# Tile-by-tile pool handover, one pass over K, and Q and K written two chunks at a time in a hybrid decoder step

## The chip, the cores and the metric

The kernel runs as one program on one core of one Trainium2 chip. The metric is the device time of one execution, in microseconds (us). Times of the kernel before and of the changed one are medians of several executions; the profile shows one more execution, recorded by the hardware profiler.

## The reference, cut to what matters

The program is one inference step of a small decoder with two layers, in float32, for a prompt of 1024 tokens and, at the same time, 8 sequences that each decode one token against 256 cached positions (two cached pages of 128 per sequence). All 1032 tokens go through the same weights.

```python
for l in range(DEPTH):                      # two layers
    if l < N_A_LAYERS:                      # layer 0: short gated convolution
        y, st = short_conv_mixer(x, conv_state[l], w_in[l], conv_w[l], w_mix_out[l])
    else:                                   # layer 1: differential attention
        kv = x @ w_kv
        k_new = partial_rope(kv[..., :QK_DIM].reshape(N, T, N_HEADS, 2, HEAD_DIM), pos)
        v_new = kv[..., QK_DIM:].reshape(N, T, N_HEADS, V_DIM)
        q = partial_rope((x @ w_q[i]).reshape(N, T, N_HEADS, 2, HEAD_DIM), pos)
        ...                                 # prompt: causal blocks; decode: past pages + new key
        a = p[:, :, 0] - lam * p[:, :, 1]   # two softmax maps per head
        o = rms_norm(a @ v, subln_g[i]) * (1.0 - lam_init)
        y = o.reshape(N, T, VO_DIM) @ w_o[i]
    x = layer_norm(DEEPNORM_ALPHA * x + y, ln1_g[l], ln1_b[l])
    x = layer_norm(DEEPNORM_ALPHA * x + swiglu(x, w_gate[l], w_up[l], w_down[l]), ln2_g[l], ln2_b[l])
```

The outputs are the new x of all tokens, k_new and v_new of all tokens, and the convolution states.

## The kernel before

**Layout.** The residual stream is held transposed: features on the 128 partitions (8 groups), tokens along the row, in four chunks of 258 tokens (CH). Chunk 3 ends with the 8 decode tokens. A float32 product is made of three products of split numbers: each operand is a high part (hi, rounded) and a low part (lo, the rest), and high x high, high x low and low x high are summed in PSUM (exact, lines 331 to 337). So one block, one chunk times one weight column group (dense, line 342), is 24 TensorE instructions of 258 columns. ScalarE makes hi by a cast (L166 for weights, L353 or L729 for data) and GpSimd (weights, L167) or VectorE (data, L354 or L730) makes lo by a subtraction.

**Weights.** A Stream (line 101) loads each half of a weight by a DMA on SP's queue into one of a few raw buffers and prepares hi and lo ahead of use into a ring. The main stream has a ring of 4; the stream of the stage that makes q, k and v has a ring of 8 and 3 raw buffers (line 1274). Resident (line 181) keeps a few weights for several uses.

**Stages.** The convolution mixer, FFN 0, then q (16 blocks for chunks 0 and 1, 16 for chunks 2 and 3), then k, then v for two of four pairs of heads, then attention by head (with the rest of v filled in), the output projection, FFN 1. K has two passes over its eight weights: chunk 3 alone, then chunks 0, 1 and 2 (line 1228). Every stage opens its own tile pools (open_pools, line 1200) in an ExitStack and closes them at its end, so that the next stage's pools lie over the same addresses. A pool opened in the default way has its tiles wait until all tiles of the earlier pools under it are released.

**q and k.** qk_op (line 743) runs one block and finishes it. Rows t = 0 and t = 1 hold the rotary halves: t = 0 is only copied (x1), t = 1 computes both rotated halves with six VectorE operations (L753 to L759). put (line 724) splits a chunk into hi and lo, in single-chunk buffers (3 of each), and writes both to DRAM on SP's queue, for k also the unsplit k (k_out). Attention later reads qh, ql, kh and kl per head.

**Decode** runs as a generator (line 826) beside the blocks of k and v: after each block side.step lets it go on until its next `yield "op"`, or for four bare yields. It gathers 16 cached K pages by indirect DMAs on GpSimd's queue (L862) into rf, which held the residual stream until that was written away to stash; multiplies each by the query (L884) and reduces it (L886); waits until the new key is complete (k_done); does a softmax; then multiplies 16 gathered V pages by their weights (L943), adds them in pairs (L947), and lets TensorE sum each pair over positions (od, L938). A gather waits until VectorE has finished with the page whose buffer it overwrites. decode_out (line 962) adds the new value, and needs all four pairs of v for the decode tokens (v_done).

**Order.** The program is written in this order, but a planner (the tile framework's scheduler, with its own costs) lays out each engine's queue from it, so an instruction can be hoisted over earlier ones of the same engine. On the chip each queue then runs strictly in the laid-out order.

Of the kernel before, what the change touches and what calls it, by code (L numbers as in the profile page):

```python
# [9 lines left out]
F32 = mybir.dt.float32  # L10
F32R = mybir.dt.float32r
# [6 lines left out]
P = 128  # L18
# [6 lines left out]
NCH = 4  # L25
HALF = ((0, 1), (2, 3))
CH = NTOK // NCH
# [209 lines left out]
def _chunk(c):  # L237
    return slice(c * CH, (c + 1) * CH)
# [3 lines left out]
def kernel(ctx: ExitStack, tc: tile.TileContext, xT, wts, prm, st, cst, dcst, rope, maskw, cache_k, cache_v,  # L242
                          page_table, y_out, k_out, v_out, conv_out):
    nc = tc.nc
    V, A, G, T, S = nc.vector, nc.scalar, nc.gpsimd, nc.tensor, nc.sync
# [34 lines left out]
    def block(items, f):  # L280
        prog.append((items, f))

    def half(*keys):
        return [("half", k) for k in keys]

    kept = {}

    def pair(key=None):

        for res in kept.values():  # L290
            if key in res.keys:
                return res.get(key)
        return [ws.take(), ws.take()]
# [4 lines left out]
    pools = {}  # L298
# [6 lines left out]
    def mm(n=CH):  # L305

        if "S" in pools:
            if not wide:
                for _ in range(2):
                    t = pools["S"].tile([P, 2, 512], F32, tag="S", name="mm2")  # L310
                    wide.extend((t[:, 0], t[:, 1]))
                wide.extend((None, None))
            t = wide.pop(0)
            if t is not None:
                return t[:, 0:n]
        t = pools["mm"].tile([P, 512], F32, tag="mm", name="mm")
        return t[:, 0:n]
# [7 lines left out]
    def tmp2():  # L325
        return pools["t2"].tile([P, CH], F32, tag="t2", name="t2")
# [15 lines left out]
    def dense(ps, w, c):  # L342

        exact(ps, [(cut(w[k // KP], k % KP), (xh[c][:, k], xl[c][:, k])) for k in range(KT)])
        return ps

    def need(c):
        g = lnq.pop(c, None)
        if g is not None:
            side.drain(g)  # L350

    def split_into(hi, lo, src):
        A.copy(out=hi, in_=src)  # L353
        V.tensor_tensor(out=lo, in0=src, in1=hi.bitcast(F32), op=ALU.subtract)  # L354

    order = {}
    tpool = None
# [139 lines left out]
    def ffn(l):  # L497
# [84 lines left out]
        final = [(n, l, f) for f in (NF - 2, NF - 1) for n in ("gate", "up")] + [("down", l, NG - 1, 0)]  # L582

        def keep_final():
            tpool.close()
            kept["ffn"] = Resident(nc, wts, tpool.enter_context(tc.tile_pool(name="kept", bufs=1)), final)

        def needs(*keys):
            return half(*[k for k in keys if k not in final])
# [128 lines left out]
    dec = {}  # L718

    def rows(t, n):  # L720

        return scr[n].rearrange("(m t i) n -> t m i n", t=8, i=8)[t]

    def put(c, t, src, which):

        hi = pools["qk"].tile([P, CH], F32R, tag="hi", name="hi")
        lo = pools["qk"].tile([P, CH], F32R, tag="lo", name="lo")
        if which == "q":
            A.activation(out=hi, in_=src, func=AF.Copy, scale=-0.125)  # L729
            V.scalar_tensor_tensor(out=lo, in0=src, scalar=-0.125, in1=hi.bitcast(F32),  # L730
                                   op0=ALU.mult, op1=ALU.subtract)
        else:
            split_into(hi, lo, src)
        S.dma_start(out=rows(t, which + "h")[:, :, _chunk(c)], in_=hi.bitcast(F32))
        S.dma_start(out=rows(t, which + "l")[:, :, _chunk(c)], in_=lo.bitcast(F32))
        if c == NCH - 1:
            V.tensor_copy(out=dec[which][:, t], in_=src[:, CH - DEC:])
            if t == 7:
                dec[which + "_done"] = True
        if which == "k":  # L740
            S.dma_start(out=k_out.rearrange("(m t i) n -> t m i n", t=8, i=8)[t][:, :, _chunk(c)], in_=src)

    def qk_op(which, t, c, w):
        need(c)
        ps = dense(mm(), w, c)
        if t == 0:
            dec["x1", c] = pools["t2"].tile([P, CH], F32, tag="x1", name="x1", bufs=2)
            A.copy(out=dec["x1", c], in_=ps)
        elif t == 1:
            x1 = dec["x1", c]  # L750
            cos, sin = dec["rope"][:, 0, _chunk(c)], dec["rope"][:, 1, _chunk(c)]
            o1, o2, t1, t2 = tmp2(), tmp2(), tmp2(), tmp2()
            V.tensor_tensor(out=t1, in0=ps, in1=sin, op=ALU.mult)  # L753
            V.tensor_tensor(out=t2, in0=ps, in1=cos, op=ALU.mult)
            V.tensor_tensor(out=o1, in0=x1, in1=cos, op=ALU.mult)
            V.tensor_tensor(out=o1, in0=o1, in1=t1, op=ALU.subtract)
            put(c, 0, o1, which)
            V.tensor_tensor(out=o2, in0=x1, in1=sin, op=ALU.mult)
            V.tensor_tensor(out=o2, in0=o2, in1=t2, op=ALU.add)  # L759
            put(c, 1, o2, which)  # L760
        elif which == "k":
            kf = tmp2()
            A.copy(out=kf, in_=ps)
            put(c, t, kf, which)
        else:
            put(c, t, ps, which)
        side.step(RATE)

    def produce(which, passes):
        def f(t, chunks):  # L770
            w = pair()
            for c in chunks:
                qk_op(which, t, c, w)
        for chunks in passes:
            for t in range(8):
                block(half((which, t)), lambda t=t, chunks=chunks: f(t, chunks))
# [49 lines left out]
    def decode():  # L826
# [23 lines left out]
        for half in range(2):  # L850
            tp = pools["st"].tile([P, 512], F32, tag="st", name="rt")
            for j in range(4):
                T.transpose(tp[0:DEC, j * P:(j + 1) * P], dec["q"][:, half * 4 + j], ident)
            A.copy(out=row.rearrange("b (m t i) -> b t m i", t=8, i=8)[:, half * 4:half * 4 + 4],
                   in_=tp[0:DEC].rearrange("b (t m i) -> b t m i", t=4, i=8))
# [18 lines left out]
        def query(b):  # L874
            A.dma_start(out=qbs[b % 2], in_=qrow_d[b].partition_broadcast(P))

        query(0)
        for j, (b, pg) in enumerate(pairs):
            if j + ahead < 16:
                gather(kv[(j + ahead) % 6], cache_k, *pairs[j + ahead])  # L880
            if pg == 0 and b + 1 < DEC:
                query(b + 1)
            t, qb = kv[j % 6], qbs[b % 2]
            V.tensor_tensor(out=t, in0=t, in1=qb, op=ALU.mult)  # L884
            yield "op" if pg else None
            V.tensor_reduce(out=sc[:, pg, 16 * b:16 * b + 16], in_=t.rearrange("p (m d) -> p m d", d=HD), axis=AX.X,  # L886
                            op=ALU.add)
        vv = kv + qbs
# [37 lines left out]
        for pg in range(2):  # L926
# [3 lines left out]
                        in_=tp[:, 0:PAST].rearrange("p (g c) -> p g c", c=2), axis=AX.X, op=ALU.add)  # L930
# [10 lines left out]
        for j, (b, pg) in enumerate(pairs):  # L941
            t = vv[j % 8].rearrange("p (h e) -> p h e", e=VD)
# [256 lines left out]

    def open_pools(stack, *specs):  # L1200
        for name, bufs, kw in specs:
            pools[name] = stack.enter_context(tc.tile_pool(name=name, bufs=bufs, **kw))

    def ffn_space(stack):

# [12 lines left out]
    def items(*parts):  # L1218
        return [i for q in parts for b in q for i in b[0]]
# [5 lines left out]
    produce("q", HALF)  # L1225
    part_q = part()
    early_q, part_q = part_q[:2], part_q[2:]
    produce("k", ((3,), (0, 1, 2)))
    fours = [half(("v", two, 0), ("v", two, 1)) for two in range(4)]
    n_k = len(prog)  # L1230
    for two in range(EARLY):
# [4 lines left out]
    part_k = part()  # L1236
# [6 lines left out]

    with ExitStack() as outer:
        open_pools(outer, ("r", 1, {}), ("s", 1, {}), ("t", 3, {}), ("mm", 6, PS), ("st", 2, PS))
        rf = pools["r"].tile([P, NCH, KT, CH], F32, name="rf")
        V.memset(eps_t, EPS)
        V.memset(mhalf, -0.5)
        A.activation(out=nlam, in_=eps_t, func=AF.Silu)
        ws = main  # L1250
        ws.start(2)
        for c in range(NCH):
            r[c] = rf[:, c]
            for k in range(0, KT, 2):
                S.dma_start(out=r[c][:, k:k + 2], in_=xT[c][:, k:k + 2])
            if c == 0:
                S.dma_start(out=prm_t, in_=prm)
                S.dma_start(out=cs, in_=cst)
                ws.start(4)
        with ExitStack() as ph:  # L1260
            open_pools(ph, ("h", 16, {}), ("u", 1, {}))
            for c in range(NCH):
                lnq[c] = side.add(load_x(c))
            run(part_a)
        with ExitStack() as ph:
            ffn_space(ph)
            run(part_f)
            kept.clear()
        with ExitStack() as ph:
            open_pools(ph, ("wb", 1, {}), ("d", 1, {}), ("t2", 5, {}), ("qk", 3, {}), ("vt", 1, {}))  # L1270
            decode_setup()
            dec["space"] = rf
            run(early_q)
            ws = Stream(nc, wts, pools["wb"], items(part_q, part_k), 8, 3)
            run(part_q)
            for c in range(NCH):
                need(c)
                S.dma_start(out=stash[c], in_=r[c])
            side.add(decode())
            dgen = side.add(decode_out())  # L1280
            run(part_k)
            side.drain(dgen)
        ws = main
# [91 lines left out]
```

## Time and profile before

| | |
|---|---|
| median of 3 executions | 2588.41 us (2587.46 to 2595.0) |
| the profiled execution | 2584.38 us |
| its span | 2582.6 us |
| TensorE (PE) busy | 2435.3 us, 94% |
| weight loads of TensorE (PEld) busy | 2374.2 us, 92% |
| VectorE (DVE) busy | 1457.1 us, 56% |
| ScalarE (ACT) busy | 981.6 us, 38% |
| GpSimd (POOL) busy | 1233.4 us, 48% |
| mean granted TensorE clock | 0.979 |

Matmuls overlap each other, so that a busy TensorE isn't TensorE at its peak; the number of matmuls in a stretch tells more. The span begins with the first instruction of the program and ends with its last. q takes from about 1123 to 1243 us of the span, k to about 1386, v to about 1437, attention to about 1713.

### The profile page before, as it was taken

How to read it: one execution, taken by the hardware profiler on the slowest of the kernel's cores; microseconds unless marked ns; L12 is line 12 of the kernel's file. 1: busy time of each engine (PE TensorE's matmuls, PEld its weight loads, DVE VectorE, ACT ScalarE, POOL GpSimd, SP SyncE). 2: the span in 40 equal slices, each digit the busy share in tenths (PEclk: the TensorE clock that was granted, in tenths of full speed). 3: DMA queues.
4: the chain of work that ended last, by engine and by line, in shares of the span. 5: the costliest groups of instructions: out<-in, count | busy, mean ns of one | idle time of the engine just before them, and what ended most of it. 6: DMA issues, size and time to landing. Idle time of an engine off the chain costs nothing. (4 is left out here: it accounts for less than half of the span.)

```text
span 2582.6 us, 49334 instructions
## 1 busy us (share of the span) xinstructions
PE 2435.3 (94%) x19482; PEld 2374.2 (92%) x19482; DVE 1457.1 (56%) x2808; ACT 981.6 (38%) x2194; POOL 1233.4 (48%) x1072
## 2 busy tenths in 40 slices
PE   8999998999999999989979799889999999999995
PEld 8999998999999999989958789789899999999995
DVE  4333877555555555595674377747854444444447
ACT  4213456322222222265322377744532222222225
POOL 4224466755555555245673243460765555555431
PEclk9999998999999999989989899999999999999997
DMA  4112342211111112157884567640311111111211
GB/s 160 50 46 87 91 137 78 72 50 52 50 50 50 50 50 94 55 165 234 270 284 150 149 177 210 171 164 18 95 58 47 49 50 50 46 50 50 92 44 66
DMA packets 149976, 252.51 MB, mean 98 GB/s; under 512 B 16840, under 2 KB 58216, under 8 KB 148592
## 3 DMA queue, kind: packets, MB, share of 16 engines
q1 hardware_dynamic: 141680, 219.75, 28.2%
q0 software_dynamic: 5456, 19.40, 2.2%
q10 hardware_dynamic: 2608, 10.20, 1.1%
q8 instruction: 153, 2.51, 0.4%
q14 instruction: 79, 0.65, 0.1%
HBM read 205.90 MB, written 43.39 MB: 97 GB/s over the span
## 5 line engine op out<-in xcount | busy, mean ns | idle before, releaser
L167 POOL TENSOR_TENSOR wlo<-raw,whi 128x512 fp32r<-128x512 f32 x482 | 643.7, 1344 | 689.1 <-ACT whi L166 516.7
L334 PE MATMUL mm<-xhf,whi 128*128 128x258 f32 x2720 | 686.3, 287 | 40.3 <-ACT xhf L403 20.5
L335 PE MATMUL mm<-xlf,whi 128*128 128x258 f32 x2720 | 682.3, 285 | 1.4 <-DVE xlf L354 0.8
L334 PEld LDWEIGHTS mm<-xhf,whi 128*128 128x128 f32 x2720 | 520.2, 191 | 47.5 <-ACT xhf L403 20.9
L335 PEld LDWEIGHTS mm<-xlf,whi 128*128 128x128 f32 x2720 | 520.4, 191 | 4.1 <-issue 1.7
L166 ACT CAST whi<-raw 128x512 fp32r<-128x512 f32 x482 | 296.4, 619 | 592.0 <-PE mm L335 406.0
L337 PE MATMUL mm<-xhf,wlo 128*128 128x258 f32 x2720 | 409.4, 285 | 13.7 <-POOL wlo L167 13.7
L337 PEld LDWEIGHTS mm<-xhf,wlo 128*128 128x128 f32 x2720 | 364.1, 192 | 16.8 <-POOL wlo L167 14.2
L334 PE MATMUL mm<-hidh,whi 128*128 128x258 f32 x1344 | 350.5, 286 | 12.9 <-DVE g L518 2.3
L335 PE MATMUL mm<-hidl,whi 128*128 128x258 f32 x1344 | 355.1, 285 | 1.7 <-DVE hidl L354 1.3
L334 PEld LDWEIGHTS mm<-hidh,whi 128*128 128x128 f32 x1344 | 251.8, 189 | 18.0 <-DVE rf L485 3.8
L337 PE MATMUL mm<-hidh,wlo 128*128 128x258 f32 x1344 | 268.3, 283 | 0.0
L335 PEld LDWEIGHTS mm<-hidl,whi 128*128 128x128 f32 x1344 | 253.6, 189 | 5.4 <-DVE hidl L354 5.3
L167 POOL TENSOR_TENSOR wlo<-ws,whi 128x512 fp32r<-128x512 f32 x108 | 139.2, 1289 | 206.4 <-ACT whi L166 203.2
L334 PE MATMUL mm<-Th,whi 128*128 128x258 f32 x864 | 218.8, 285 | 4.7 <-DVE m L546 4.7
L335 PE MATMUL mm<-Tl,whi 128*128 128x258 f32 x864 | 217.6, 283 | 0.0
L337 PEld LDWEIGHTS mm<-hidh,wlo 128*128 128x128 f32 x1344 | 208.4, 190 | 0.0
L485 DVE TENSOR_TENSOR rb<-mm,rb 128x258 f32<-128x258 f32 x320 | 134.2, 425 | 102.5 <-PE mm L337 102.2
L485 DVE TENSOR_TENSOR rf<-mm,rf 128x258 f32<-128x258 f32 x352 | 143.0, 422 | 68.1 <-PE mm L337 67.6
L334 PEld LDWEIGHTS mm<-Th,whi 128*128 128x128 f32 x864 | 163.8, 190 | 6.9 <-DVE m L546 6.6
L335 PEld LDWEIGHTS mm<-Tl,whi 128*128 128x128 f32 x864 | 163.2, 189 | 0.0
L166 ACT CAST whi<-ws 128x512 fp32r<-128x512 f32 x108 | 67.0, 620 | 232.8 <-PE mm L335 204.5
(240 smaller groups left out, 4371.7 us busy)
## 6 DMA issues: line engine op xcount, KB each, us to landing
raw<-in_wts SPq DMA_DIRECT2D x482, 256.0 KB
rraw<-in_wts SPq DMA_DIRECT2D x36, 256.0 KB
qh<-qh SPq DMA_DIRECT2D x60, 128.0 KB
ql<-ql SPq DMA_DIRECT2D x60, 128.0 KB
rf<-in_xT SPq DMA_DIRECT2D x16, 258.0 KB
stash<-rf SPq DMA_DIRECT2D x4, 1032.0 KB
qh<-hi SPq DMA_DIRECT2D x32, 129.0 KB
ql<-lo SPq DMA_DIRECT2D x32, 129.0 KB
```

What stands on the lines that cost most here:

```text
L166: nc.scalar.copy(out=hi, in_=src)
L167: g.tensor_tensor(out=lo, in0=src, in1=hi.bitcast(F32), op=ALU.subtract)
L334: T.matmul(ps, lhsT=wh, rhs=h, start=(first and i == 0), stop=False, **kw)
L335: T.matmul(ps, lhsT=wh, rhs=l, start=False, stop=False, **kw)
L337: T.matmul(ps, lhsT=wl, rhs=h, start=False, stop=(last and i == len(terms) - 1), **kw)
L485: V.tensor_tensor(out=R[:, n], in0=ps, in1=R[:, n], op=ALU.add)
```

## The change

- Every pool that open_pools opens, and the pool of the kept FFN weights, gets reuse_waits="tile": a tile then waits only for the earlier tiles whose addresses it takes over.
- K is made in one pass over its weights, in the chunk order 2, 3, 0, 1. The two decode-only v blocks that were placed among the last of the 16 K weights are placed among the last of 8.
- q and k go through buffers of two chunks (duo): hi, lo and the unsplit row (sf) are tiles of two chunks, two of each, and one DMA writes two chunks. For k these are three DMAs per pair of chunks in place of six, for q two in place of four.
- Decode gives up its turn after each cached K page's product, not after every second.
- Buffers: x1 2 to 4, t2 5 to 2, qk from 3 single ones to 2 double ones, the weight ring of the stage 8 to 7.

```diff
-            kept["ffn"] = Resident(nc, wts, tpool.enter_context(tc.tile_pool(name="kept", bufs=1)), final)
+            kept["ffn"] = Resident(nc, wts, tpool.enter_context(tc.tile_pool(name="kept", bufs=1, reuse_waits="tile")), final)
...
+    def duo(tag, c, t):
+
+        if c % 2 == 0:
+            dec[tag, t] = pools["qk"].tile([P, 2, CH], F32 if tag == "sf" else F32R, tag=tag, name=tag)
+        return dec[tag, t][:, c % 2]
+
     def put(c, t, src, which):
 
-        hi = pools["qk"].tile([P, CH], F32R, tag="hi", name="hi")
-        lo = pools["qk"].tile([P, CH], F32R, tag="lo", name="lo")
+        hi, lo = duo("hi", c, t), duo("lo", c, t)
...
-        S.dma_start(out=rows(t, which + "h")[:, :, _chunk(c)], in_=hi.bitcast(F32))
-        S.dma_start(out=rows(t, which + "l")[:, :, _chunk(c)], in_=lo.bitcast(F32))
         if c == NCH - 1:
             V.tensor_copy(out=dec[which][:, t], in_=src[:, CH - DEC:])
-            if t == 7:
-                dec[which + "_done"] = True
-        if which == "k":
-            S.dma_start(out=k_out.rearrange("(m t i) n -> t m i n", t=8, i=8)[t][:, :, _chunk(c)], in_=src)
+        if c % 2:
+            toks = slice((c - 1) * CH, (c + 1) * CH)
+            todo = [(rows(t, which + n[0]), dec[n, t].bitcast(F32)) for n in ("hi", "lo")]
+            if which == "k":
+                todo.append((k_out.rearrange("(m t i) n -> t m i n", t=8, i=8)[t], dec["sf", t]))
+            for out, tile_ in todo:
+                S.dma_start(out=out[:, :, toks], in_=tile_.rearrange("p a n -> p (a n)"))
 
     def qk_op(which, t, c, w):
...
-            dec["x1", c] = pools["t2"].tile([P, CH], F32, tag="x1", name="x1", bufs=2)
+            dec["x1", c] = pools["t2"].tile([P, CH], F32, tag="x1", name="x1", bufs=4)
...
-            o1, o2, t1, t2 = tmp2(), tmp2(), tmp2(), tmp2()
+            o1, o2, t1, t2 = duo("sf", c, 0), duo("sf", c, 1), tmp2(), tmp2()
...
-            kf = tmp2()
+            kf = duo("sf", c, t)
...
+        if t == 7 and c == NCH - 1:
+            dec[which + "_done"] = True
         side.step(RATE)
...
             V.tensor_tensor(out=t, in0=t, in1=qb, op=ALU.mult)
-            yield "op" if pg else None
+            yield "op"
...
-            pools[name] = stack.enter_context(tc.tile_pool(name=name, bufs=bufs, **kw))
+            pools[name] = stack.enter_context(tc.tile_pool(name=name, bufs=bufs, reuse_waits="tile", **kw))
...
-    produce("k", ((3,), (0, 1, 2)))
+    produce("k", ((2, 3, 0, 1),))
...
-            open_pools(ph, ("wb", 1, {}), ("d", 1, {}), ("t2", 5, {}), ("qk", 3, {}), ("vt", 1, {}))
+            open_pools(ph, ("wb", 1, {}), ("d", 1, {}), ("t2", 2, {}), ("qk", 2, {}), ("vt", 1, {}))
...
-            ws = Stream(nc, wts, pools["wb"], items(part_q, part_k), 8, 3)
+            ws = Stream(nc, wts, pools["wb"], items(part_q, part_k), 7, 3)
```

## Rows read from the trace of the kernel before

**Rows 1.** The page: its span and part 1, busy us of each engine.

```profile
span 2582.6 us, 49334 instructions
...
PE 2435.3 (94%) x19482; PEld 2374.2 (92%) x19482; DVE 1457.1 (56%) x2808; ACT 981.6 (38%) x2194; POOL 1233.4 (48%) x1072
```

**Rows 2.** Busy time in stretches; columns stand in the first line.

```profile
core 0: us, PE busy (x) PEld busy (x) DVE busy (x) ACT busy (x) POOL busy (x), PEclk, DMA share, GB/s
...
1125.80:1137.60 11.80, 0.00 (x0) 0.00 (x0) 11.77 (x13) 8.37 (x17) 7.25 (x6) 0.63 0.70 221
...
1181.00:1243.50 62.50, 62.50 (x524) 62.41 (x522) 23.56 (x49) 27.57 (x58) 30.93 (x23) 1.00 0.72 212
...
1260.00:1272.00 12.00, 7.90 (x59) 7.07 (x58) 10.15 (x11) 4.53 (x10) 7.51 (x5) 1.00 0.99 308
...
1300.00:1312.00 12.00, 7.09 (x57) 6.67 (x56) 11.97 (x16) 2.55 (x7) 9.82 (x8) 1.00 1.01 351
...
1329.00:1341.50 12.50, 0.83 (x8) 0.62 (x6) 10.32 (x13) 2.71 (x7) 10.80 (x2) 0.69 0.16 43
...
1386.50:1437.50 51.00, 50.49 (x433) 49.48 (x431) 5.57 (x7) 9.41 (x23) 7.46 (x10) 1.00 0.21 66
1437.50:1457.50 20.00, 6.61 (x26) 4.63 (x26) 2.46 (x14) 2.31 (x9) 5.07 (x10) 0.64 1.01 251
...
1705.00:1727.00 22.00, 16.41 (x118) 15.96 (x117) 5.85 (x12) 8.54 (x14) 18.28 (x15) 0.84 0.87 307
```

**Rows 3.** TensorE's waits, 1122 to 1244: us in total, times, longest.

```profile
PE mm L334 <- ACT xhf L403: 11.9, 1, 11.9
```

**Rows 4.** TensorE's waits, 1244 to 1386.

```profile
PE mm L337 <- POOL wlo L167: 13.7, 2, 11.7
```

**Rows 5.** TensorE in order of time, 1436 to 1458: start, us, instruction, idle before.

```profile
1447.30 0.55 PE L1033 MATMUL S<-tk,qh 128*128 128x256 f32 x1 [8.13 <-issue]
...
1454.26 0.55 PE L1034 MATMUL S<-tk,ql 128*128 128x256 f32 x1 [3.58 <-DMA ql<-ql]
```

**Rows 6.** ScalarE in order of time, 1116 to 1139 (ACTq: its queue).

```profile
1119.90 0.35 ACTq L811 DMA_DIRECT2D rope_t<-in_rope  x1
...
1128.97 1.93 ACT L166 CAST whi<-raw 128x512 fp32r<-128x512 f32 x3 [2.79 <-DMA raw<-in_wts]
```

**Rows 7.** Groups by line, 1243.5 to 1386.5: busy us, mean ns, idle before.

```profile
L167 POOL TENSOR_TENSOR wlo<-raw,whi 128x512 fp32r<-128x512 f32 x37 | 53.8, 1462 | 32.8 <-ACT whi L166 31.5 <-ACT sd L905 0.6 <-issue 0.4
...
L884 DVE TENSOR_TENSOR rf<-rf 128x1024 f32<-128x1024 f32 x16 | 23.2, 1482 | 0.0
...
L354 DVE TENSOR_TENSOR lo<-t,hi 128x258 fp32r<-128x258 f32 x32 | 21.1, 679 | 9.2 <-ACT hi L353 7.8 <-DMA kl<-lo 1.4
L886 DVE TENSOR_REDUCE sc<-rf 128x16 f32<-128x1024 f32 x16 | 19.0, 1205 | 0.0
L938 PE MATMUL od<-rf,sel 128*8 128x512 f32 x32 | 16.4, 650 | 0.0
...
L947 DVE TENSOR_TENSOR rf<-rf 128x1024 f32<-128x1024 f32 x8 | 11.8, 1469 | 0.1
```

**Rows 8.** GpSimd, then VectorE, in order of time near 1330.

```profile
1330.63 9.53 POOL L862 DMA_INDIRECT rf<-in_cache_v,idx  x1 [5.96 <-DVE rf L947]
...
1338.11 1.21 DVE L947 TENSOR_TENSOR rf<-rf 128x1024 f32<-128x1024 f32 x1
```

**Rows 9.** VectorE's V products (L943) alone, 1320 to 1372.

```profile
1320.00:1372.00 52.00, 23.07 (x16) 0.87 0.72 248
```

**Rows 10.** VectorE in order of time, 1143 to 1162.

```profile
1146.55 7.89 DVE L755 TENSOR_TENSOR t<-x,rope_t 128x258 f32<-128x258 f32 x1
...
1159.98 0.41 DVE L755 TENSOR_TENSOR t<-x,rope_t 128x258 f32<-128x258 f32 x1
```

**Rows 11.** GpSimd in order of time, 1408 to 1449.

```profile
1434.45 0.64 POOL L1001 DMA_DIRECT2D tk<-kh  x1 [14.92 <-PE vps L788]
```

## The prediction, made before the changed kernel was run

> **What bounds the kernel now.** First the page: TensorE is busy for 2435.3 of the 2582.6 us of the span [rows 1], so only what makes TensorE wait counts. The change removes no matmul. So I read the list of TensorE's waits for the three stages that the diff touches, then a table of those stages in stretches. In the steady part of the q stage 524 matmuls take 62.50 us [rows 2]: 0.119 us each, 2.86 us for a block of 24 (one chunk by one weight). The time lost in any other stretch of 258-column products is its length less 0.119 us for each matmul in it. The reader is to see five places in rows 2:
> - 1125.8 to 1137.6: 11.8 us, no matmul. TensorE waits for the cast of x after a layer norm [rows 3]; the clock fell to 0.63.
> - 1260 to 1272: 59 matmuls, 7.0 us of work in 12: 5.0 us lost.
> - 1300 to 1312: 57 matmuls, 6.8 us in 12: 5.2 us lost, VectorE busy for 11.97 of it.
> - 1329 to 1341.5: 8 matmuls, 1.0 us in 12.5: 11.5 us lost, waiting for one wlo [rows 4]; clock 0.69.
> - 1437.5 to 1457.5, the start of attention: 6.61 us busy in 20, clock 0.64. TensorE waits 8.13 us at the first score and 3.58 us for ql [rows 5].
>
> A sixth is 1705 to 1727, where 118 matmuls are 14.0 us of work in 22: 8 us lost.
>
> **The change part by part. A: the start of q.** The rope table's load (1 MB) is issued at 1119.90, and the weight cast behind it gets its data at 1128.97, 2.79 us late [rows 6], in the middle of the layer norm chain for which TensorE waits. Today every tile of the new pools waits for the last tile of the old ones; with the change the rope tile, which by the sizes lies over the first kept FFN weights, waits for these alone and can go some microseconds earlier. Its 1 MB would then not collide with the first weights of q. The rest of the chain (sqrt, reciprocal, scale, affine, cast) stays. I take -3 us, near the late weight cast; the ends are 0 (the chain is as long without it) and -9 (most of the stall).
>
> **B: one K pass.** Now weights are prepared twice, for chunk 3 alone and then for chunks 0 to 2. Of the 37 preparations in this stage [rows 7] sixteen go: 16 x 1.46 = 23 us of GpSimd, as many casts, 4 MB of loads. In the pass of chunk 3 a pair of preparations, 2.9 us of GpSimd, serves one 2.86 us block: GpSimd has no slack, and the 5.0 us lost at 1260 are weight waits. With four chunks a pair serves 11.5 us. I take -5 (ends -5 and 0).
>
> **C: decode's V part leaves the K stage.** The 11.5 us at 1329 come from a gather of a V page on GpSimd's queue that took 9.53 us [rows 8], while VectorE multiplied and added V pages back to back; the wlo that TensorE needed stood behind it. Decode needs the new key of all eight weights for chunk 3 (k_done). Today that is so after 8 of the 32 K blocks, after the change at the 30th, so the V pages are worked on beside the products of v. There all eight preparations of v's two passes are written ahead of the gathers in the program (a ring of 7, four taken at once), so nothing that TensorE needs soon stands behind a gather. -11.5, and -1 for the slow clock after it: -12.5 (ends -13 and 0, if the same gather blocks the next weights).
>
> What it adds in the v stage: that stage is 433 matmuls in 51.00 us now [rows 2], and gets the 32 od products, 16.4 us [rows 7], which only move. Beside them stands VectorE with the 16 V pages, 23.07 us [rows 9], and 8 adds, 11.8 us [rows 7]. They took most of the window of 52 us today [rows 9], more than their 35 us of work, since they waited for gathers; in 67 us they fit with little to spare. TensorE waits at each of the eight sums if VectorE is late: I take +2, ends 0 and +12 (one gather like the long one).
>
> By the Trainium skill, "SBUF — State Buffer", section "Who interferes with whom", VectorE and GpSimd share one port pair as an exclusive lock, held for a whole instruction, and descriptors of a GpSimd DMA can't be written meanwhile. Rows 8 agree in kind, not in size: an operation of VectorE took 1.21 us there, the gather 9.53. The rule speaks against the change: the gathers of V meet the same adds in the v stage. That is the first rival.
>
> **D: one cached page per product.** Now two K pages go with each block of 24 matmuls, later one. A page costs VectorE 1.48 + 1.21 = 2.69 us, the lo of a chunk 0.68 [rows 7]: with two pages 6.1 us per block against 2.86 of TensorE, with one 3.4. But the one pass puts the rope of all four chunks where the pages begin (block 5): six operations of 0.41 [rows 10] and two lo's are 3.8 us, 6.5 with the page. For blocks 5 to 20 VectorE has 4 x 6.5 + 12 x 3.4 = 67 us against 46 us of TensorE, 21 us of lag. It is taken up by six PSUM banks (17 us) and the two pair buffers, and worked off in blocks 21 to 32. About 5 us of stall, as at 1300 today: 0, ends -5 and +21.
>
> **E: pairs of chunks in one write.** Three DMAs per pair replace six; SP issues half as many. A buffer was needed again three blocks after its write began; with two pair buffers it is again three blocks. 0, ends -3 and +5. Ring 8 to 7 is hidden by B's halved demand; t2's 5 to 2 buffers by the sf tiles. Both 0, and each costs part of E's +5 without that cover.
>
> **F: the start of attention.** Its first loads are issued at 1434.45, GpSimd having waited for the last products of v [rows 11], and the first score starts at 1447.30 [rows 5]. With tile waits the K and Q tiles, which lie over rf, wait for decode's last read of rf, which C puts some 50 us into a 67 us stage. The loads then have about 15 us under v's products; 13 passed today from the first issue to the first score. The pipeline of softmax must still fill. -10, ends 0 and -15.
>
> **G: the start of the output projection.** The resident weights load as soon as their own addresses are free: -2 of the 8 us, ends 0 and -6. The other pool changes (before either FFN) lie under matmuls or wait for norms: 0, ends -3 and +3. A planner orders each engine's instructions anew, which I can't price; the ends of the parts hold it.
>
> **The sum:** -3 - 5 - 12.5 + 2 + 0 + 0 - 10 - 2 = -30.5 us. The profiled execution took 2584.38 us (2582.6 of span and 1.8 around it), so 2553.9 by its own time. The median of the runs shown is 4.0 higher, 2588.41: 2557.9, and 2558 is the forecast for a median.
>
> **Rivals.** *V ends late.* The gathers starve in the v stage as at 1330: decode runs to the end of v or past it, rf comes free as late as the pools do now, F is nothing and C's added wait is +12. Sum -3 - 5 - 12.5 + 12 - 2 = -10.5: 2578. For it: the 52 us for 35 us of work; against: six of the sixteen gathers are issued before the products start.
> *The pools were not what held.* A, F and G bring nothing, because data (norms, k and v written to DRAM) or a queue's order hold the loads as late. -5 - 12.5 + 2 = -15.5: 2573. For it: rows 3 name a norm, not a pool. Against: the GpSimd wait of 14.92 us ends on a product of v [rows 11], and in the program K is complete before v's last two passes begin.
> *Decode paces TensorE* (slower). The place is block 5 onward of the single K pass. A pair buffer comes free only after VectorE's second lo and the landing of its write; if the lag holds both buffers, ScalarE can't empty PSUM and TensorE runs at VectorE's pace: +21 instead of 0, and the clock falls in these stops as it did to 0.69. If GpSimd's preparations also hold VectorE, as when one multiply of 0.41 us took 7.89 [rows 10], twice, that is 15 more. The late K stage leaves F nothing, and C's wait is +12. Sum -3 - 5 - 12.5 + 12 + 21 + 15 - 2 = +25.5: 2614. It decides from a lag of about 26 us (PSUM's 17 and one pair buffer's three blocks); my sum says 21.
> *It goes better:* A whole (-9), C without the +2, F -14, G -5: -46.5, 2542.
>
> **How the numbers follow.** The forecast holds with a chance of 0.50 (its own range 2547 to 2569), V late 0.14, the pools 0.14, paced by decode 0.12, better 0.10. A measurement of this kernel tells about 0.3% from no change, 7.8 us: faster is below 2580.6. From the cases: faster 0.50 + 0.10 + 0.09 + 0.11 = 0.80; the rest of the V and pool cases and a little of the pacing case give no difference, 0.10; slower 0.10. The range for 8 in 10 is 2538 to 2588: it reaches over V late and the pools and leaves out most of the pacing case.
>
> **What would show it.** A: the rope load issued before 1119, and a gap of under 10 us before the second q block. B: 16 fewer wlo, no wait for whi early in K. C: no wait of TensorE for wlo above 5 us in K or v; the V multiplies beside v's products, with gathers in between. D: VectorE near 100% in the first 20 blocks of K, TensorE's waits for sf there about 5 us in sum. F: the first tk load issued over 8 us before the last product of v, and under 5 us from that product to the first score. The prediction is wrong if these waits go and others of like size come (od products waiting for VectorE, hi or sf waiting for a write), or if attention's loads still wait for the end of v.

## The result and the profile after

The changed kernel takes 2565.1 us (median of 4 executions, 2562.01 to 2567.36) against 2590.17 of the kernel before (4 executions on the same chips): a ratio of 0.990, 95% interval 0.9881 to 0.992. The forecast was 2558, with a range of 2538 to 2588. The two profiled executions, 2584.38 before and 2566.27 after, differ by 18.1 us only, because the profiled one of before lies 5.8 us under its median and that of the changed kernel 1.2 over its own. Stage by stage the two traces differ by this (from the start of a stage's first matmul, us; the first decode product, lps, stands behind the second block of K):

| stretch | before | after | difference |
|---|---|---|---|
| start of the span to the first decode product beside K | 1243.5 | 1242.9 | -0.6 |
| from there to the last product of v ahead of attention ("K and v") | 195.6 | 191.1 | -4.5 |
| from there to the first score | 8.1 | -0.2 | -8.3 |
| first score to the output projection | 267.8 | 262.8 | -5.0 |
| output projection to the end of the span | 867.5 | 867.8 | +0.3 |

(-0.2: the first score starts under the last product of v.) TensorE is as busy as before [rows 1], in a shorter span:

```profile
span 2564.5 us, 49008 instructions
...
PE 2433.6 (95%) x19482; PEld 2376.8 (93%) x19482; DVE 1439.6 (56%) x2808; ACT 973.2 (38%) x2178; POOL 1206.0 (47%) x1056
```

The stretches of the changed kernel that answer to [rows 2], with the same columns:

```profile
1126.80:1140.20 13.40, 0.01 (x1) 0.02 (x1) 10.98 (x17) 8.42 (x17) 7.42 (x6) 0.67 0.75 230
...
1260.00:1272.00 12.00, 12.00 (x102) 12.00 (x101) 12.00 (x13) 2.58 (x5) 5.92 (x5) 1.00 0.66 211
1272.00:1292.00 20.00, 6.16 (x42) 5.73 (x42) 19.54 (x31) 1.46 (x4) 14.48 (x10) 0.74 0.99 372
1292.00:1304.00 12.00, 8.23 (x39) 8.03 (x38) 12.00 (x14) 3.31 (x10) 9.47 (x5) 0.64 0.95 319
1374.00:1434.00 60.00, 58.73 (x400) 44.47 (x399) 27.11 (x25) 8.67 (x20) 22.96 (x24) 1.00 0.50 156
1434.00:1450.00 16.00, 14.80 (x98) 12.65 (x97) 11.76 (x40) 10.35 (x29) 5.50 (x6) 1.00 0.79 200
...
1687.00:1709.00 22.00, 16.73 (x118) 16.12 (x116) 4.55 (x11) 7.91 (x13) 17.11 (x15) 0.84 0.78 277
```

The stall ahead of q is still there. The loss at 1260 is gone (102 matmuls in 12 us), and so is the one before the first score (14.80 us busy of 16 at full clock, where before 6.61 of 20 at 0.64). In their place stands one new hole: 81 matmuls, 9.6 us of work, in the 32 us from 1272 to 1304, VectorE busy for 31.5 of them. TensorE's waits in K, 1246 to 1374, no longer name a weight [rows 4]:

```profile
PE mm L334 <- DVE t L760: 13.8, 2, 13.6
PE mm L334 <- ACT sf L769: 3.8, 1, 3.8
```

VectorE in order of time there (L759 and L760 are the two rope products that read PSUM, L892 and L894 the two operations of a K page):

```profile
1258.65 2.36 DVE L892 TENSOR_TENSOR rf<-rf 128x1024 f32<-128x1024 f32 x2 [3.07 <-DMA rf<-qrow_d]
...
1272.49 0.42 DVE L759 TENSOR_TENSOR t<-mm,rope_t 128x258 f32<-128x258 f32 x1
...
1286.77 0.41 DVE L759 TENSOR_TENSOR t<-mm,rope_t 128x258 f32<-128x258 f32 x1
...
1287.43 1.21 DVE L894 TENSOR_REDUCE sc<-rf 128x16 f32<-128x1024 f32 x1
1288.56 1.21 DVE L892 TENSOR_TENSOR rf<-rf 128x1024 f32<-128x1024 f32 x1
1289.70 0.41 DVE L760 TENSOR_TENSOR t<-mm,rope_t 128x258 f32<-128x258 f32 x1
```

From 1258.65 to 1289.70 VectorE works off 21 page operations (11 of L892, 10 of L894), and the rope products stand in line among them. The first of the four rope blocks was complete at 1253, the fourth three blocks of 2.86 us later, at 1261.6; the read that frees its PSUM bank ends at 1290.1, 28.5 us later. TensorE filled the five other banks (14.3 us) and then stood for 13.6.

GpSimd, then TensorE, at the end of v and the start of attention, for [rows 11, 5]:

```profile
1377.39 3.97 POOL L870 DMA_INDIRECT rf<-in_cache_v,idx  x1 [14.99 <-DVE rf L955]
...
1414.58 0.64 POOL L1009 DMA_DIRECT2D tk<-kh  x1
...
1433.88 0.28 PE L1041 MATMUL S<-tk,qh 128*128 128x256 f32 x1
```

Attention's first load is issued 19.9 us earlier than before and 19.3 us ahead of the first score, which follows v without a gap.

### The profile page after: what moved, and what is told of

The parts are those of the page before. It is cut to its first block, busy times and chain, and to the rows that moved or that the text cites. A ratio compares the mean times of both kernels' runs of the same rounds, so it can differ in the third digit from the quotient of the medians.

```text
span 2564.5 us, 49008 instructions
## 1 busy us (share of the span) xinstructions
PE 2433.6 (95%) x19482; PEld 2376.8 (93%) x19482; DVE 1439.6 (56%) x2808; ACT 973.2 (38%) x2178; POOL 1206.0 (47%) x1056
## 5 line engine op out<-in xcount | busy, mean ns | idle before, releaser
L167 POOL TENSOR_TENSOR wlo<-raw,whi 128x512 fp32r<-128x512 f32 x466 | 619.2, 1338 | 713.7 <-ACT whi L166 501.0
L166 ACT CAST whi<-raw 128x512 fp32r<-128x512 f32 x466 | 286.6, 619 | 594.6 <-PE mm L335 423.6
```

Of the source, the lines that this page charges most:

```text
L166: nc.scalar.copy(out=hi, in_=src)
L167: g.tensor_tensor(out=lo, in0=src, in1=hi.bitcast(F32), op=ALU.subtract)
```

## The experiments

Theory 1: the gain comes from the V pages that left the K stage, from the single pass and from the tile waits at the start of attention; decode's K pages beside the rope of four chunks take part of it back. Each run is compared with the kernel before on the same chip (medians there 2588.96 to 2591.53 us, so two changed kernels from two chips compare to within some 2.6 us). "K and v" is the second stretch of the table above.

**Default waits.** The changed kernel without its pool edit:

```diff
-tc.tile_pool(name=name, bufs=bufs, reuse_waits="tile", **kw)
+tc.tile_pool(name=name, bufs=bufs, **kw)          # and the same for "kept"
```

> The changed kernel with the pools' default waits put back in both places (all else as changed). Theory 1: the tile waits are worth the early start of attention and nothing else, so the first score waits again for loads issued after the last product of v, as before the change: about 13 us back, 2578 us. Rival: attention starts early because decode and K end in another order, not because of the waits: 2565 us, the first K load still issued some 19 us before the first score. If the waits also carried the start of q and of the output projection by some microseconds each, 2583.

2580.28 us, ratio 0.9963 (0.995 to 0.9976). GpSimd and TensorE in order of time:

```profile
1428.08 0.65 POOL L1009 DMA_DIRECT2D tk<-kh  x1 [14.77 <-PE vps L796]
...
1441.37 0.55 PE L1041 MATMUL S<-tk,qh 128*128 128x256 f32 x1 [8.59 <-DMA out_v<-vt]
...
1448.54 0.55 PE L1042 MATMUL S<-tk,ql 128*128 128x256 f32 x1 [3.84 <-DMA ql<-ql]
```

The loads wait for a product of v again, and the two waits of [rows 5] are back (8.59 and 3.84 us). Without the tile waits the rest of the change is worth 8.9 us of the 25.

**Waits only.** The kernel before with that edit alone.

> The kernel before with the tile waits in both places and nothing else of the change. Theory 1: decode's V pages are worked off in the K stage here, so the space under attention's tiles is free well before v ends; the first score comes some 12 us earlier, and the loss at the end of K (one wlo, 11.5 us) stays: 2578 us. Rival, that the waits work only with the later parts of the change: 2590 us, the first K load issued at the last product of v as before.

2568.62 us, ratio 0.9921 (0.9908 to 0.9934): 20.5 us, more than the 11 expected. The first load of attention goes out 19 us ahead of the first score, which starts at the end of v (GpSimd, then TensorE, in order of time):

```profile
1417.97 0.64 POOL L1001 DMA_DIRECT2D tk<-kh  x1
...
1437.08 0.28 PE L1033 MATMUL S<-tk,qh 128*128 128x256 f32 x1
```

K and v are as long as before (195.5), with the wait of 11.67 us for one wlo in place. The start of attention is thus worth more than its gap of 8.1 us: the wait for ql, and the clock of 0.64 in this stretch, go with it (attention 262.1 us for 267.8). Gap and attention make 14.0 us of the 15.5 by which the two profiled executions differ; the rest of the 20.5 between the medians no trace shows.

**Pages held in the program.** The decode generator yields until the rope of the last chunk has been written down:

```diff
+        if which == "k" and t == 1 and c == 1:
+            dec["rope_done"] = True
...
+        while "rope_done" not in dec:
+            yield "op"
         for j, (b, pg) in enumerate(pairs):
```

> The changed kernel with decode's 16 K pages held back until the rope of all four chunks is done (they start at K block 9 instead of 5). Theory 1: the two waits of 13.64 and 3.77 us at 1290 to 1303 come from VectorE doing rope and pages at once; held back, VectorE has 4 x 3.8 us in four blocks of 2.86 (4 us of lag) and then 3.4 us a block for 16 blocks (9 us more), which six PSUM banks cover: both waits go, 15 to 17 us, 2549 us. Rival, that the two pair buffers and their writes hold the rope's results: the first wait stays near 14 us and the time at 2565. Rival, that the lag is only moved: a wait of like size some 35 us later, 2562 to 2570.

2564.73 us, ratio 0.9896 (0.9881 to 0.9912): the changed kernel's time. TensorE's first wait in K (us in total, times, longest):

```profile
PE mm L334 <- DVE t L760: 12.9, 1, 12.9
```

VectorE in order of time (L896 is a page's product):

```profile
1254.29 2.36 DVE L896 TENSOR_TENSOR rf<-rf 128x1024 f32<-128x1024 f32 x2 [2.56 <-DMA rf<-qrow_d]
...
1281.84 0.41 DVE L759 TENSOR_TENSOR t<-mm,rope_t 128x258 f32<-128x258 f32 x1
...
1284.77 0.42 DVE L760 TENSOR_TENSOR t<-mm,rope_t 128x258 f32<-128x258 f32 x1
```

This doesn't decide between theory 1 and its rivals, since nothing moved: the first page starts as soon as its query row has landed and VectorE's instructions stand in the same order. The place of a `yield` didn't set the order on the chip here; the planner hoists what has its data.

**V pages held in the program, and by data.** In the kernel before, the V part is held back to the 30th K block, first by a loop of yields, then by data:

```diff
+        if which == "k" and t == 7 and c == 0:
+            dec["k_late"] = True
...
-        while "k_done" not in dec:
+        while "k_late" not in dec:
```

> The kernel before with one edit: decode's V pages wait for the 30th of K's 32 blocks, as in the changed kernel, instead of the 8th; pools, passes and writes as before. Theory 1: the wait of 11.5 us for one wlo at 1329 goes with its slow clock, and the v stage takes the V pages for 2 us or less: 2578 to 2580 us. Rival, that the V pages cost as much beside the products of v: waits of od products for VectorE of some 10 us, 2590 us or above, and attention's start later.

2588.83 us, ratio 0.9998 (0.9989 to 1.0007). Here too the V pages stay in the K stage (only the decode sums od come later); the long gather returns (GpSimd in order of time), and with it the wait of TensorE for wlo (second fence):

```profile
1334.47 9.53 POOL L864 DMA_INDIRECT rf<-in_cache_v,idx  x1 [4.82 <-DVE rf L949]
...
1345.45 0.96 POOL L864 DMA_INDIRECT rf<-in_cache_v,idx  x1 [0.16 <-issue]
```

```profile
PE mm L337 <- POOL wlo L167: 12.8, 2, 11.3
```

The second form, a run of its own, adds at the same place a true dependency:

```diff
+            V.scalar_tensor_tensor(out=dec["k"][:, 0, 0:1], in0=kf[:, 0:1], scalar=0.0,
+                                   in1=dec["k"][:, 0, 0:1], op0=ALU.mult, op1=ALU.add)
```

> The kernel before with decode's V part made to depend on the 30th K block by data (an element of the new keys takes 0 times that block's result), so that its V pages cannot be worked on in the K stage; everything else as before. Theory 1: the 9.53 us gather beside VectorE's adds no longer stands before a wlo that K needs, the wait of 11 to 12 us for it goes, and v takes the pages for 2 us or less: K and v 186 instead of 195.6 us, 2578 to 2580 us. Rival (the V pages cost as much wherever they lie): od products or wlo wait some 10 us in v, 2587 or above.

2585.51 us, ratio 0.999 (0.9981 to 0.9999). The waits of TensorE, 1244 to 1436 (us in total, times, longest):

```profile
PE mm L334 <- DVE t L754: 5.6, 1, 5.6
PE mm L334 <- ACT whi L166: 5.3, 5, 1.4
PE vps L792 <- ACT whi L166: 3.5, 2, 2.6
...
PE mm L337 <- POOL wlo L167: 1.4, 1, 1.4
```

The wait for wlo is gone as forecast (12.8 to 1.4), yet K and v are 195.7 us long, as before. Of the 12.3 us that the wait for wlo lost against [rows 4] (13.7 to 1.4), 6.8 came back as waits for whi (2.0 to 8.8), 2.5 as waits of the od sums and 1.4 as waits in the rope. Taken alone, moving the V pages gives 3 us in the medians, at the edge of the interval, and no trace shows where: of the two profiled executions this one is the slower (2588.12 against 2584.38).

**Pages after the rope, by data.** To the changed kernel with its pages held in the program, as above, this is added, so that the first two query rows need the last rope result:

```diff
+            if j in (0, 2):
+                V.scalar_tensor_tensor(out=qb[:, 0:1], in0=dec["sf", 1][:, 1, 0:1], scalar=0.0,
+                                       in1=qb[:, 0:1], op0=ALU.mult, op1=ALU.add)
             V.tensor_tensor(out=t, in0=t, in1=qb, op=ALU.mult)
```

> The changed kernel with a true data dependency: the first two query rows take 0 times an element of the last chunk's rope result, so no K page can be multiplied before the rope of all four chunks is through, wherever the planner would put it. Theory 1 (VectorE did rope and pages at once): the two waits of 13.64 and 3.77 us go, with the slow clock after them; the rope's four blocks cost VectorE some 4 us of lag, the pages follow at 2.4 us against 2.86 of a block: K and v 15 us shorter, 2550 us. Rival (pair buffers and their writes): a wait of 10 us or more stays at the fourth chunk, 2562 to 2566. Rival (lag only moved): waits of like sum for sf or od later, 2560 or above.

2552.57 us, ratio 0.9863 (0.9848 to 0.9878); K and v 176.2 us, 14.9 less than in the changed kernel. The waits of TensorE that are left in K (us in total, times, longest):

```profile
PE vps L798 <- ACT whi L166: 4.3, 1, 4.3
...
PE mm L337 <- POOL wlo L167: 1.2, 1, 1.2
```

VectorE in order of time (the last read of the fourth rope block, and the first pages), and after it a stretch with the columns of [rows 2]:

```profile
1262.75 0.43 DVE L760 TENSOR_TENSOR t<-mm,rope_t 128x258 f32<-128x258 f32 x1
...
1265.39 4.62 DVE L899 TENSOR_TENSOR rf<-rf 128x1024 f32<-128x1024 f32 x4
```

```profile
1272.00:1292.00 20.00, 20.00 (x169) 20.00 (x168) 19.29 (x20) 6.63 (x17) 14.71 (x12) 1.00 1.01 379
```

The fourth chunk's bank is free at 1263.2 instead of 1290.1, and TensorE runs 169 matmuls in the stretch in which the changed kernel ran 42, although VectorE is as full (19.29 us of 20). So it wasn't VectorE's load that stopped TensorE, but which instruction waited in its queue. This and the run with later V gathers below have the lowest medians.

**Three pair buffers, and their control.** The changed kernel with three buffers per pair and a ring of 5 for room; then with the ring of 5 alone.

> The changed kernel with three buffers instead of two for each pair (hi, lo, sf), and a weight ring of 5 instead of 7 to make room. Rival (the pair buffers and their writes hold the rope back): both waits in K shrink to under 5 us together, 2552 us. Theory 1 (VectorE is full from 1258 to 1305 whatever the buffers): the first wait stays within 2 us of 13.64, at most the second (3.77, for sf) goes: 2561 to 2566.

> The changed kernel with a weight ring of 5 instead of 7 and the pair buffers left at two: the control for the run with three buffers, which had the waits in the rope down to 5.9 us but 9.4 us of new waits for whi, and K and v as long as the changed kernel's (192.1 against 191.1). Theory 3 (both buffers and VectorE's order make the stall; the shorter ring gave the gain back): K and v some 8 us longer than the changed kernel's, 2570 to 2575, with the waits of 13.64 and 3.77 us still there. Rival (the third buffer only moved the stall to the weights): K and v at 191 to 193, whi waits as small as in the changed kernel, 2565.

2557.96 us (ratio 0.9885, 0.987 to 0.99) and 2560.45 us (0.9882, 0.9866 to 0.9898). TensorE's waits, three buffers first:

```profile
PE vps L796 <- ACT whi L166: 6.4, 2, 5.7
PE mm L334 <- ACT sf L769: 4.6, 2, 3.1
PE mm L334 <- ACT whi L166: 3.0, 2, 1.6
...
PE mm L334 <- DVE t L760: 1.3, 2, 0.9
```

```profile
PE mm L334 <- DVE t L760: 12.5, 1, 12.5
PE mm L334 <- ACT sf L769: 5.2, 1, 5.2
```

With three buffers the wait for the rope all but goes (1.3 us), against theory 1. The fourth rope bank is still held for 27.7 us (1254.6 to 1282.3; 28.5 in the changed kernel), but TensorE runs seven blocks in that time for five. The difference is in ScalarE, whose copies (L769) empty the banks of the next weight's blocks into a pair buffer; its first ones, in the changed kernel and with three buffers:

```profile
1298.93 0.65 ACT L769 COPY sf<-mm 128x258 f32<-128x258 f32 x2 [5.11 <-DMA out_k<-sf]
```

```profile
1272.46 0.38 ACT L769 COPY sf<-mm 128x258 f32<-128x258 f32 x1 [7.55 <-DVE sf L764]
```

With two buffers, both taken by the rope, none of the five other banks is emptied before TensorE stands. So the stall needs both: pages ahead of the rope products, and two pair buffers.

K and v stay at 192.1 us all the same: the time turns up as waits for whi (9.4 us) and sf (4.6). The control has no wait for whi in K (190.9 us), against what theory 3 forecast for it. But there TensorE still stands 12.5 us for the rope, in which weights are prepared, so this does not clear the ring of 5; the last two runs below show what it costs without that stall. Both kernels come to K earlier than the changed one (first decode product at 1235.9 and 1237.1 for 1242.9). Why was not settled; a part may be spread between executions, since the run with pages held in the program has the ring of 7 and comes to K at 1239.3.

**Two passes again.** The kernel with pages after the rope, its V part also held by data, and K's weights prepared twice:

```diff
-    produce("k", ((2, 3, 0, 1),))
+    produce("k", HALF[::-1])
```

> The kernel of the run with pages after the rope (2552.6 us, K and v 176.2 us), with K's weights prepared in two passes again (chunks 2 and 3, then 0 and 1), the K pages after the first pass's rope and the V part held to the 31st block by data: 16 more weight preparations and 4 MB more of loads in the K stage, the rest the same. The forecast's size for the single pass (B): 5 us, 2557. Theory 2: the DMA engines are full there (share 0.94 to 1.03 from 1270 to 1330 at some 400 GB/s), so 4 MB are 10 us and TensorE waits for casts of weights (whi) by that: K and v 186 us, 2562. Rival: the loads fit in the gaps and GpSimd has slack: 2553.

2568.01 us, ratio 0.9911 (0.9896 to 0.9926): 15.4 us more than with one pass (13.0 when each is taken against the kernel before on its own chip), K and v 193.8 us. These passes take two chunks each, where the kernel before took one and three. TensorE's waits for whi in K and v and what the casts waited for from 1285 to 1340, then a stretch with the columns of [rows 2]:

```profile
PE mm L334 <- ACT whi L166: 10.9, 6, 4.9
PE vps L802 <- ACT whi L166: 5.1, 3, 2.3
...
ACT whi L166 <- DMA raw<-in_wts: 10.6, 5, 3.5
```

```profile
1280.00:1300.00 20.00, 15.65 (x111) 15.24 (x110) 18.22 (x18) 5.32 (x14) 14.86 (x10) 0.84 1.03 394
```

GpSimd has room (14.86 us of 20), the DMA engines have none (1.03). The 16 preparations cost about three times what the forecast took, and a third to a half more than theory 2's 10 us: the waits are 11.7 us longer, and a lower clock (0.84 in this stretch) comes on top. No run had more raw buffers than 3, so whether loads issued earlier would have hidden this is open.

**Later V gathers.** To the kernel with pages after the rope: the page numbers of V take 0 times a result of the 28th K block.

```diff
+        if which == "k" and t == 6 and c == 1:
+            dec["tick"] = dp1 = pools["d"].tile([P, 1], F32, name="tick")
+            V.scalar_tensor_tensor(out=dp1, in0=kf[:, 0:1], scalar=0.0, in1=dec["cst"][:, 2:3],
+                                   op0=ALU.mult, op1=ALU.add)
```

> The kernel of the run with pages after the rope, with the gathers of V pages made to depend by data on the 28th K block, so that no V page (3 MB of six) is fetched while the DMA engines are full. Theory 2 (the last waits in K, 4.33 us for whi and 1.17 for wlo, are the DMA engines'): these go, 2548 us, unless the first V page comes so late that the products of od wait. Rival: the waits stay, since the query rows and k's writes fill the engines alone, and V's pages end later: 2553 to 2557.

2551.92 us, ratio 0.9851 (0.9834 to 0.9867): not to be told from 2552.57; K and v 179.8 us. The waits of K and v:

```profile
PE od L962 <- DVE rf L971: 3.0, 1, 3.0
PE aT L951 <- DVE sd L942: 2.5, 1, 2.5
...
PE mm L334 <- ACT whi L166: 0.9, 1, 0.9
```

The wait for whi went from 4.3 to 0.9 us, as theory 2 says, and K ends earlier (98.5 us after its first decode product for 101.1); but decode's later V part now makes the products of aT and od wait (2.5 and 3.0 us), and nothing is left over.

**Shorter ring and third buffer on top.** Pages after the rope with the ring of 5, then with three pair buffers too.

> Pages after the rope by data (2552.6 us) together with the weight ring of 5 (which took 4.6 us off the changed kernel, some 3 of it in the q stage, where the loss from 1160 to 1180 fell from 2.5 to 1.3 us of wait and the clock from 0.91 to 1.00). If the two are independent: 2548 us, K and v still 176. Rival (with the K stage no longer stalled, the shorter ring shows as waits for whi there): K and v 182 or more, 2553 to 2557.

> The same with three buffers for each pair too. In the q stage the last wait between 1160 and 1180 goes (as in the run with three buffers): 1.3 us more. In K the rope has its slack, so a third buffer has nothing to hold: K and v 176, 2546 us. Rival (as in the run with three buffers on the changed kernel, TensorE runs ahead into waits for whi while the DMA engines are full): K and v 180 or more, 2550.

2557.99 us (ratio 0.987, 0.9849 to 0.989) and 2555.4 us (0.9855, 0.983 to 0.9879), K and v 187.1 and 183.3 us: the rivals, both times, by K and v; the ratios themselves are not to be told from 0.9863. With the rope stall gone a ring of 5 is too short for K: it waits for whi by 7.9 and 9.1 us in sum, 4.3 with the ring of 7. The run with three buffers waited for whi by 9.4, which points to the ring of 5 as what took back there what the third buffer gave, as theory 3 had it; no run has three buffers with a ring of 7.

## Why the prediction was right, and where its steps were not

The time fell inside the forecast's own range (2547 to 2569) and 7 us above its middle: the gain was 25.1 us for 30.5, and the median of before came out 1.8 higher. That it came so near is in part luck, since the terms were less right than their sum. By the table of stages, K and v became 4.5 us shorter, where B, C and D make 15.5, and the gap ahead of attention with attention itself 13.3, where F makes 10. Where the kernels compared ran on two chips, the next table has two numbers: by the medians as they are, and with each kernel taken against the kernel before on its own chip.

| part | forecast | measured |
|---|---|---|
| A, start of q | -3 | 0: the gap is 13.4 us for 11.9 [rows 3] |
| B, one K pass | -5 | -15.4 or -13.0, with decode's pages held off the rope |
| C, V pages out of K | -10.5 | -3 alone, seen in no trace |
| D, K pages beside the rope | 0 | +12.5 or +11.3 |
| F, start of attention | -10 | -20.5 alone (14.0 seen in the traces), -15.2 or -16.2 as the last part |
| G, output projection | -2 | 0 |

*A* failed as a mechanism. The rope load is issued at 1118.12 for 1119.90 [rows 6], and the gap in the other kernels is 10.1 to 11.9 us with either kind of wait. The cast after the layer norm ends it each time, so no pool is shown to set it.

*B* had the right sign and too small a size. It was priced on GpSimd, whose 2.9 us per pair met a block of 2.86, and so on the 5.0 us lost at 1260. TensorE's waits there, 1256 to 1274 of the kernel before, name GpSimd's wlo and the casts before it about equally:

```profile
PE mm L337 <- POOL wlo L167: 2.1, 1, 2.1
PE mm L334 <- ACT whi L166: 2.0, 3, 1.3
```

The DMA engines, for whose loads the casts waited in the run with two passes, were full: their share stood in [rows 2], 0.99 and 1.01 in the two lossy stretches of K, and was not used.

*C* was right in where the 11.5 us came from (the wait for wlo goes when the V pages leave, and returns with the same gather of 9.53 us when they don't), and wrong that the time is then gained: with two passes more than half of it is waited for weights instead. B and C can't be priced apart. From the kernel before to the one with two passes and both kinds of page held by data (and with the pair writes and tile waits) K and v become 1.8 us shorter, and the single pass then takes off another 17.6.

*D* is the largest miss. Its sum of VectorE's work (a lag of 21 us, as a balance over 16 blocks, against some 26 that banks and buffers take up) was if anything too high: a page took 2.42 us in K, not 2.69. But a bank is held by one instruction, not by a balance. Because the planner puts pages ahead of the rope products as soon as their data is there, the fourth chunk's bank was held for 28.5 us, and the 14.3 us of five other banks were the only cover. The slower rival (decode paces TensorE) named the rest of it: both pair buffers held, ScalarE unable to empty PSUM. It came with a stall of 17.4 us where it took 21; its other prices did not: no TensorE wait in K names a preparation, the V pages fit beside v (od waits 0.8 us there) and F stayed whole. The prediction's own sign of being wrong, waits that go while others of like size come, is thus met in K (17.6 us of waits for 21.1). One page per `yield` was taken for the pace of the chip; the two holds in the program show that it isn't.

*F* was the forecast's best reading: the load behind a product of v [rows 11], 8.13 us at the first score, and the wait for ql. It was under-sized: the slow clock of this stretch was not counted. The rival that the pools were not what held falls with the first two runs for F; for A and G it was right. (The better case's parts add up to 45.5 us, not 46.5.)

*E* was not run by itself. *V ends late* did not come: the one long gather of the v stage took 3.97 us. By the Trainium skill, "SBUF — State Buffer", section "Who interferes with whom", a GpSimd DMA that an operation of VectorE stalls is short of port time to make its descriptors; of tensor_tensor, the operation of these adds and multiplies, the section says that it contends with GpSimd's reads, and infers that it leaves the descriptors alone. The rows here show the stall beside tensor_tensor: 9.53 us beside back-to-back adds and multiplies, twice, and 0.96 us when VectorE was idle, and the measurement decides. What of the gather was held, no run here shows.

Left open: what three pair buffers give with a ring of 7, and what the shorter ring does ahead of K.

## What to carry to other kernels

Before a stall is priced on the engine that is named, read the DMA share of the same stretch: where it was at 1, a wait that was taken away came back in part as others, and loads that were dropped were worth more than the engine time they freed. When side work shares an engine with the work that frees PSUM, ask how long a single bank is held, and whether the others can be emptied meanwhile, not whether the balance of work fits; and order it by a data dependency, since the holds in the program left the pages where they were. Removing a wait at a stage's start can be worth more than its gap (here 14.0 us for 8.1, with a second wait and a slow clock behind it).

## What the runs showed of the hardware

The time from issue to landing of a weight load of 256 KB, in the kernel with pages after the rope, first from 1190 to 1235 (DMA share about 0.66), then from 1265 to 1315 (1.0):

```profile
DMA to landing us min/median/max: 3.2/3.8/4.9
...
DMA to landing us min/median/max: 4.8/10.7/14.8
```

A load takes three times as long where the engines are full. At 371 to 403 GB/s (1272 to 1324) they deliver the 4.2 MB of 16 loads in 10 to 11 us; the kernel with two passes has 11.7 us more of waits for whi than the one with a single pass (16.0 and 4.3).
